# A decoder trunk on one core: the second product of the MLPs by a seven-product scheme in three of four chunks

## The chip, the core and the metric

The kernel runs on one core of one Trainium2 chip. The metric is the device time of one execution in microseconds (us), as the median of several runs. TensorE (PE) multiplies, VectorE (DVE), ScalarE (ACT) and GpSimd (POOL) work on tensors in SBUF, SyncE (SP) issues most DMAs. PSUM has eight banks, each of 128 partitions by 512 float32.

## The reference

The trunk has two layers on 512 tokens of width 1024: attention and retention as token mixers, each followed by a squared-ReLU MLP of width 4096 and a gated embedding. What the change touches is the MLP and what is added behind it:

```python
def sq_relu_mlp(xn, w1, w2):
    h = jax.nn.relu(xn @ w1)
    return (h * h) @ w2
...
        x = x + mix
        x = x + sq_relu_mlp(rms_norm(x, norm_mlp[i]), mlp_w1[i], mlp_w2[i])
        gate = jax.nn.sigmoid(rms_norm(x, norm_pe[i]) @ pe_w_gate[i])
        x = x + gate * (p[i] @ pe_w_up[i])
```

## The kernel before

Activations stand transposed: a tile is 128 features by 512 tokens. Every float32 operand of a product is split into a high half (rounded to the type that TensorE multiplies) and a low half (the remainder); `mm3` makes each product of three passes: high by high (L187), high by low (L188), low by high (L189). A pass loads 128x128 weights and streams 512 columns of tokens.

Weights come through the class `Weights`. `order` lists all weight tiles (128x1024) in the order of their use. `next()` hands out tile i and calls `load()` until four tiles beyond it are under way. `load()` fetches the tile by SP's queue into one of three buffers `raw`, ScalarE casts it to `wh` (L83), VectorE subtracts for the remainder `wl` (L87); of each half there are five buffers. From the first attention products until the middle of the first MLP's first chunk the remainder is made by a DMA instead (`by_dma`).

`mlp` walks over four chunks of 1024 hidden features. In the hidden stage eight tiles of 24 passes go to banks `ph` (three buffers, tag mm). `end` empties a bank: VectorE takes the maximum with 0 times `rsm` (`ht`, L644), ScalarE squares and casts to `hh`, VectorE makes `hl` (L165). In the second product eight output tiles of 24 passes go to banks `py`, and VectorE adds each to the residual `x[m]` (L654). The first chunk of an MLP starts with two tiles side by side, since the row sums for `rsm` come late (`tiles`, `late`).

In each layer the embedding product `p @ pe_w_up` is made early: for layer 0 it waits in DRAM (`up0`) and `back` reads it into `put` by SP's queue; for layer 1 it waits in SBUF, in eight tiles `pus` of the pool `zp`. `gated_embedding` uses it in `end` (L698) and, in the last layer, stores `x[m]` by SP's queue (L701); its last tile goes in two halves of 256 columns.

The order of instructions on each engine is set by a scheduler from the program's order, its buffers and dependencies; each engine then works through its own list strictly in that order.

Of the kernel before, what the change touches and what calls it, by code (L numbers as in the profile page):

```python
# [10 lines left out]
F32 = mybir.dt.float32  # L11
# [5 lines left out]
P = 128  # L17
# [34 lines left out]
class Weights:  # L52
# [3 lines left out]
    def __init__(self, tc, pool, order, ahead):  # L56
        self.tc, self.nc, self.pool, self.order, self.ahead = tc, tc.nc, pool, order, ahead
        self.made = []
        self.at = 0
        self.lo_engines = (self.nc.vector,)  # L60
        self.parts = 1
        self.by_dma = False

    def load(self):
        nc = self.nc
        i = len(self.made)
        src = self.order[i]
        raw = self.pool.tile([P, 1024], F32, name=f"raw{i}", tag="raw", bufs=RAW_BUFS)
# [32 lines left out]
def decoder_trunk(ctx: ExitStack, tc, xT, pT, small, dist, decay, ident,  # L101
# [10 lines left out]
    def ps_mm(name):  # L112
        return psum("mm", 3, name)
# [17 lines left out]
    def gate_order(up, g):  # L131
        return [up[0], up[1]] + [g[i] for i in range(8)]

    order = []
# [5 lines left out]
    for c in range(4):  # L140
        order += [w1_0[8 * c + i] for i in range(8)]
        order += [w2_0[8 * c + i] for i in range(8)]
    order += [w_g0[i] for i in range(8)]
    for h in range(RH):
        order += [w_rv[4 * h + i] for i in range(4)]
# [6 lines left out]
    for c in range(4):  # L152
        order += [w1_1[8 * c + i] for i in range(8)]
        order += [w2_1[8 * c + i] for i in range(8)]
    order += [w_g1[i] for i in range(8)]

    W = Weights(tc, gp, order, W_BUFS - 1)
# [147 lines left out]


    dp = ctx.enter_context(tc.tile_pool(name="dp", bufs=1, space=bass.MemoryType.DRAM))
    up0 = dp.tile([KD // 2, P, 2, T], F32, name="up0")


    with tc.tile_pool(name="at", bufs=1) as ap:
# [314 lines left out]
    def mlp(z, acc, layer, late_at=2):  # L626
        late, rs = rs_rows(acc, f"rsm{layer}")
        nacc = None
        zn = []
        with tc.tile_pool(name=f"mlp{layer}", bufs=1) as mp:  # L630
            for c in range(4):
                hs = []

                def begin(f):
                    if (layer, c, f) == (0, 0, 4):
                        W.by_dma = False
                    return W.next(), ps_mm(f"ph{layer}{c}{f}")

                def unit(s, f, k):
                    mm3(s[1], cols(s[0], slice(k * P, k * P + P)), z[k], k == 0, k == KD - 1)  # L640

                def end(s, f):
# [5 lines left out]
                tiles(8, begin, unit, end, late if c == 0 else None, late_at)  # L648
                for m in range(KD):
                    w = W.next()  # L650
                    ps = ps_mm(f"py{layer}{c}{m}")
                    for f in range(8):
                        mm3(ps, cols(w, slice(f * P, f * P + P)), hs[f], f == 0, f == 7)
                    nc.vector.tensor_tensor(out=x[m], in0=x[m], in1=ps, op=ALU.add)  # L654
                    if c == 3:
                        if m == 0:
                            nacc = slot(f"acc_p{layer}")
                        zn.append(make_z(x[m], C_PE + 8 * layer, m))
                        squares(nacc, x[m], m)
        return zn, nacc  # L660

    def gated_embedding(z, acc, p, layer, last, make=slot, made=None):
# [45 lines left out]
            tiles(KD, begin, unit, end, late)  # L708
        return zn, st["acc"]

    with tc.tile_pool(name="zp", bufs=1) as zp:

        def zslot(name, dt):
            return zp.tile([P, T], dt, name=name, tag="z", bufs=16)

        def back(pool, m):
            t = pool.tile([P, T], F32, name="put", tag="put", bufs=4)
            load(t, up0[m // 2][:, m % 2, :])
            return t

        z, acc = mlp(z, acc, 0)
        z, acc = gated_embedding(z, acc, None, 0, False, zslot, made=back)


        late, rs = rs_rows(acc, "rsr")
        zn = []
        with tc.tile_pool(name="ret", bufs=1) as ap:
# [229 lines left out]
```

## Time and profile before

| | |
|---|---|
| runs, median (lowest to highest) | 1474.82 us (1474.77 to 1479.93), 3 runs |
| the profiled execution, its own time | 1477.73 us |
| its span | 1476.0 us |
| TensorE busy | 1456.2 us (99%), 6668 passes recorded |
| weight loads busy | 1195.0 us (81%) |
| VectorE busy | 787.9 us (53%) |
| ScalarE busy | 648.7 us (44%) |
| GpSimd busy | 155.2 us (11%) |
| chain that ended last, share of TensorE | 91% |

The span is the time from the first to the last instruction in the profiled execution. Busy times are unions, since recorded passes overlap; a TensorE that is busy throughout is not thereby at its peak.

### The profile page before, as it was taken

The numbers are of one execution on the slowest core, as the hardware profiler recorded it, in microseconds if no ns is written. First come the engines' busy times: TensorE is split into PE (matmuls) and PEld (weight loads), VectorE is DVE, ScalarE is ACT, GpSimd is POOL, SyncE is SP. The second block draws the span as 40 slices with busy tenths as digits, with TensorE's granted clock in tenths as the row PEclk, the third lists the DMA queues.
The fourth block names the chain that finished last, engine by engine and source line by source line (L and its number), as shares of the span: only waits on it lengthen the run. The fifth ranks groups of instructions, "written<-read, shape, count | busy, mean of one in ns | idle before, by whom it ended". The sixth has DMA issues, their size and how long they took to land.

```text
span 1476.0 us, 17128 instructions
## 1 busy us (share of the span) xinstructions
PE 1456.2 (99%) x6668; PEld 1195.0 (81%) x6668; DVE 787.9 (53%) x1189; ACT 648.7 (44%) x1007; POOL 155.2 (11%) x127
## 2 busy tenths in 40 slices
PE   9999999999999999999999999999999999999998
PEld 7777667888888888888888888888878888888887
DVE  6776677643434434485464555553684343434455
ACT  6777777742323223354442532433552231323432
POOL 4112112100000000310120200301220000000020
PEclk9999999999999999999999999999999999999999
DMA  6654566853333333244223133142233333333312
GB/s 227 143 115 115 129 170 142 216 158 100 100 90 96 100 101 98 65 152 134 66 88 112 64 101 93 57 129 71 84 102 100 92 94 100 100 98 91 98 58 86
DMA packets 46880, 159.92 MB, mean 108 GB/s; under 512 B 5200, under 2 KB 5712, under 8 KB 46800
## 3 DMA queue, kind: packets, MB, share of 16 engines
q1 hardware_dynamic: 41328, 138.92, 30.1%
q0 software_dynamic: 4896, 17.83, 6.7%
q10 hardware_dynamic: 576, 2.10, 0.4%
q8 instruction: 52, 0.85, 0.2%
q14 instruction: 28, 0.23, 0.0%
HBM read 136.80 MB, written 4.19 MB: 96 GB/s over the span
## 4 chain that ended last, share of the span: by engine, by line
PE 91%; DVE 3%; ACT 2%; DMA 2%; issue 1%; POOL 0%; SPq 0%; ACTq 0%; POOLq 0%; DVEq 0%
PE py L187 8%; PE py L188 8%; PE py L189 8%; PE ph L188 8%; PE ph L187 8%; PE ph L189 8%; PE rg L187 2%; PE rg L188 2%; PE pg L189 2%; PE pg L188 2%; PE pg L187 2%; PE rv L188 2%; PE rqk L188 2%; PE rv L189 2%; PE rqk L189 2%; PE rv L187 2%
## 5 line engine op out<-in xcount | busy, mean ns | idle before, releaser
L83 ACT CAST wh<-raw 128x1024 fp32r<-128x1024 f32 (+1 forms) x211 | 221.0, 1049 | 602.7 <-PE py L188 235.7
L87 DVE TENSOR_TENSOR wl<-raw,wh 128x1024 fp32r<-128x1024 f32 (+1 forms) x211 | 266.8, 1265 | 55.0 <-ACT wh L83 54.0
L188 PE MATMUL ph<-zl,wh 128*128 128x512 f32 x512 | 199.4, 390 | 0.1
L187 PE MATMUL ph<-zh,wh 128*128 128x512 f32 x512 | 199.2, 389 | 0.0
L189 PE MATMUL ph<-zh,wl 128*128 128x512 f32 x512 | 199.2, 389 | 0.0
L187 PE MATMUL py<-hh,wh 128*128 128x512 f32 x512 | 199.2, 389 | 0.0
L188 PE MATMUL py<-hl,wh 128*128 128x512 f32 x512 | 199.2, 389 | 0.0
L189 PE MATMUL py<-hh,wl 128*128 128x512 f32 x512 | 199.2, 389 | 0.0
L654 DVE TENSOR_TENSOR x<-x,py 128x512 f32<-128x512 f32 x64 | 44.0, 688 | 200.0 <-PE py L189 200.0
L644 DVE SCALAR_TENSOR_TENSOR ht<-ph,rsm 128x512 f32<-128x512 f32 x64 | 44.1, 691 | 158.3 <-PE ph L189 158.0
L188 PEld LDWEIGHTS ph<-zl,wh 128*128 128x128 f32 x512 | 96.1, 188 | 20.6 <-DVE zl L168 0.9
L187 PEld LDWEIGHTS ph<-zh,wh 128*128 128x128 f32 x512 | 96.1, 188 | 20.1
L189 PEld LDWEIGHTS py<-hh,wl 128*128 128x128 f32 x512 | 96.1, 188 | 20.1
L189 PEld LDWEIGHTS ph<-zh,wl 128*128 128x128 f32 x512 | 96.1, 188 | 20.0
L187 PEld LDWEIGHTS py<-hh,wh 128*128 128x128 f32 x512 | 96.1, 188 | 20.0
L188 PEld LDWEIGHTS py<-hl,wh 128*128 128x128 f32 x512 | 96.1, 188 | 19.8
L237 POOL TENSOR_TENSOR acc_p<-acc_p,sq 128x512 f32<-128x512 f32 x14 | 24.2, 1726 | 649.0 <-ACT sq L236 649.0
L187 PE MATMUL pqk<-wh,zh 128*128 128x512 f32 x128 | 51.7, 404 | 1.7 <-ACT qkt L368 1.7
L188 PE MATMUL pqk<-wl,zh 128*128 128x512 f32 x128 | 50.9, 398 | 0.8 <-DMA wl<-raw 0.8
L187 PE MATMUL pg<-zh,wh 128*128 128x512 f32 (+1 forms) x136 | 51.2, 377 | 0.0
L189 PE MATMUL pg<-zh,wl 128*128 128x512 f32 (+1 forms) x136 | 51.2, 377 | 0.0
L188 PE MATMUL pg<-zl,wh 128*128 128x512 f32 (+1 forms) x136 | 51.2, 376 | 0.0
(870 smaller groups left out, 2776.8 us busy)
## 6 DMA issues: line engine op xcount, KB each, us to landing
raw<-in_w SPq DMA_DIRECT2D x128, 512.0 KB, 3.6
wl<-raw POOLq DMA_DIRECT2D x34, 512.0 KB, 5.3
raw<-in_w_qk SPq DMA_DIRECT2D x16, 512.0 KB, 3.8
raw<-in_w_g SPq DMA_DIRECT2D x16, 512.0 KB, 3.7
raw<-in_w_rv SPq DMA_DIRECT2D x16, 512.0 KB, 3.7
raw<-in_w_rqk SPq DMA_DIRECT2D x16, 512.0 KB, 4.2
raw<-in_w_rg SPq DMA_DIRECT2D x16, 512.0 KB, 3.6
raw<-in_w_ro SPq DMA_DIRECT2D x16, 512.0 KB, 3.7
```

Of the source, the lines that this page charges most:

```text
L83: nc.scalar.copy(out=hi[:, s], in_=raw[:, s])
L87: e.tensor_tensor(out=lo[:, r], in0=raw[:, r], in1=hi[:, r].bitcast(F32), op=ALU.subtract)
L187: nc.tensor.matmul(ps, a[0], b[0], start=start, stop=False)
L188: nc.tensor.matmul(ps, a[0], b[1], start=False, stop=False)
L189: nc.tensor.matmul(ps, a[1], b[0], start=False, stop=stop)
L237: (engine or nc.gpsimd).tensor_tensor(out=acc, in0=acc, in1=sq, op=ALU.add)
L644: nc.vector.scalar_tensor_tensor(out=t, in0=s[1], scalar=0.0, in1=rs, op0=ALU.max, op1=ALU.mult)
L654: nc.vector.tensor_tensor(out=x[m], in0=x[m], in1=ps, op=ALU.add)
```

## The change

In the first three of four chunks of each MLP the second product is made by a scheme of seven block products for eight. Hidden features, output features and tokens are each cut in two. A round covers four output tiles (two rounds a chunk). Weight blocks are a11, a12, a21, a22 (each 128x1024 here: two tiles j by 512), and

- s1 = a21 + a22 (VectorE), s2 = s1 - a11, s4 = a12 - s2, s3 = a11 - a21 in place of a21 (GpSimd),
- of the hidden activations seven parts of 256 tokens: the four quarters and four sums `hu` (VectorE),
- seven products of 24 passes with 256 columns, accumulated in banks b, c, a; after each product VectorE adds the bank as it stands to a half of an `x` tile.

`MIX` lists the products in their order: name, bank, part of the hidden activations, and the half tile to which the bank is then added. In a chunk's first round the last quarter (q = 3) of s1 and s2 is put behind their other three. The hidden tiles come in pairs (tile f and f + 4). The second layer's embedding product now waits in DRAM (`up1`), stored by ScalarE's queue and read by `back`.

```diff
+MIXED = 3
+MIX = (
+    ("a11", "b", 0, (0, 0)),
+    ("s1", "c", 3, (1, 1)),
+    ("s2", "b", 5, (0, 1)),
+    ("s4", "c", 2, (0, 1)),
+    ("s3", "b", 4, (1, 1)),
+    ("a12", "a", 1, (0, 0)),
+    ("a22", "b", 6, (1, 0)),
+)
...
+    def mixed(self, kind, w, first):
...
+        def fetch(b):
+            raw = self.pool.tile([P, 1024], F32, name=f"raw{i}_{b}", tag="raw", bufs=RAW_BUFS)
+            src = w[first + b // 2 : first + b // 2 + 3 : 2, :, b % 2 * T : b % 2 * T + T].rearrange("j p n -> p j n")
+            self.tc.keep_in_program_order(nc.sync.dma_start(out=raw.rearrange("p (j n) -> p j n", j=2), in_=src))
+            return raw
+
+        def fresh():
+            return self.sums.tile([P, 1024], F32, name=f"mix{i}", tag="mix", bufs=2)
+
+        if kind == "a11":
+            t = mix["a11"] = fetch(0)
+        elif kind == "s1":
+            mix["a21"], a22 = fetch(2), fetch(3)
+            t = mix["s1"] = fresh()
+            nc.vector.tensor_tensor(out=t, in0=mix["a21"], in1=a22, op=ALU.add)
+        elif kind == "s2":
+            t = mix["s2"] = fresh()
+            nc.gpsimd.tensor_tensor(out=t, in0=mix["s1"], in1=mix["a11"], op=ALU.subtract)
+        elif kind == "s4":
+            mix["a12"] = fetch(1)
+            t = fresh()
+            nc.gpsimd.tensor_tensor(out=t, in0=mix["a12"], in1=mix["s2"], op=ALU.subtract)
+        elif kind == "s3":
+            t = mix["a21"]
+            nc.gpsimd.tensor_tensor(out=t, in0=mix["a11"], in1=t, op=ALU.subtract)
+        elif kind == "a12":
+            t = mix["a12"]
+        else:
+            t = fetch(3)
+        hi = self.pool.tile([P, 1024], F32R, name=f"wh{i}", tag="wh", bufs=W_BUFS)
+        lo = self.pool.tile([P, 1024], F32R, name=f"wl{i}", tag="wl", bufs=W_BUFS)
+        nc.scalar.copy(out=hi, in_=t)
+        nc.vector.tensor_tensor(out=lo, in0=t, in1=hi.bitcast(F32), op=ALU.subtract)
+        return hi, lo
...
+            def products(n, j, first, last):
+                kind, b, part, (tile, half) = MIX[n]
...
+                ps = bank[b, j][:, 0 : T // 2]
+                for q in range(first, last):
+                    mm3(
+                        ps, cols(ws[n], slice(j * T + q * P, j * T + q * P + P)),
+                        tuple(p[:, part, :] for p in hs[q]), n == opens[b] and q == 0, q == 3, n != opens[b],
+                    )
+                if last == 4:
+                    t = x[4 * r + 2 * j + tile][:, half * (T // 2) : (half + 1) * (T // 2)]
+                    nc.vector.tensor_tensor(out=t, in0=t, in1=ps, op=ALU.add)
...
-                    t = mp.tile([P, T], F32, name="ht", tag="ht", bufs=3)
-                    nc.vector.scalar_tensor_tensor(out=t, in0=s[1], scalar=0.0, in1=rs, op0=ALU.max, op1=ALU.mult)
-                    nc.scalar.activation(out=t, in_=t, func=AF.Square)
-                    hs.append(hilo(mp, "h", t, bufs=10))
...
+                    if c >= MIXED:
+                        put(2 * second, 2, half)
+                    elif not second:
+                        put(0, 1, t[:, 0:1, :])
+                    else:
+                        put(1, 2, half)
+
+                        u = mp.tile([P, 4, T // 2], F32, name="hu", tag="hu", bufs=1)
+                        nc.vector.tensor_tensor(out=u[:, 0:2, :], in0=t[:, 1:4:2, :], in1=t[:, 0:2, :], op=ALU.subtract)
+                        nc.vector.tensor_tensor(out=u[:, 2, :], in0=t[:, 3, :], in1=u[:, 0, :], op=ALU.subtract)
+                        nc.vector.tensor_tensor(out=u[:, 3, :], in0=t[:, 2, :], in1=u[:, 2, :], op=ALU.subtract)
+                        put(3, 4, u)
...
-                t = zslot(f"pus{m}", F32)
                 nc.scalar.copy(out=t, in_=pu)
-                made.append(t)
+                nc.scalar.dma_start(out=up1[m // 2][:, m % 2, :], in_=t)
...
-        gated_embedding(z, acc, None, 1, True, made=lambda pool, m: made[m])
+    gated_embedding(z, acc, None, 1, True, made=back(up1))
```

Three places show how the lists of instructions change. The first is VectorE's list in the hidden stage of the first MLP's second chunk (chunk 1), from tile 5 to tile 7 (`ph015` to `ph017`); before:

```order
L644 SCALAR_TENSOR_TENSOR ht_3803<-ph015_3778,rsm0_3005 128x512
L87 TENSOR_TENSOR wl60_3812<-raw60_3810,wh60_3811 128x1024
L165 TENSOR_TENSOR hl_3807<-ht_3803,hh_3806 128x512
L644 SCALAR_TENSOR_TENSOR ht_3841<-ph016_3816,rsm0_3005 128x512
L87 TENSOR_TENSOR wl61_3850<-raw61_3848,wh61_3849 128x1024
L165 TENSOR_TENSOR hl_3845<-ht_3841,hh_3844 128x512
L644 SCALAR_TENSOR_TENSOR ht_3879<-ph017_3854,rsm0_3005 128x512
```

and now:

```order
L233 TENSOR_TENSOR hl_3993<-ht_3991,hh_3992 128x256
L759 SCALAR_TENSOR_TENSOR ht_3991<-ph015_4008,rsm0_3003 128x512
L145 TENSOR_TENSOR wl66_4046<-mix66_4043,wh66_4045 128x1024
L777 TENSOR_TENSOR hu_4037<-ht_3991 128x512
L233 TENSOR_TENSOR hl_3993<-ht_3991,hh_3992 128x512
L778 TENSOR_TENSOR hu_4037<-ht_3991,hu_4037 128x256
L779 TENSOR_TENSOR hu_4037<-ht_3991,hu_4037 128x256
L233 TENSOR_TENSOR hl_3993<-hu_4037,hh_3992 128x1024
L759 SCALAR_TENSOR_TENSOR ht_4074<-ph016_4049,rsm0_3003 128x512
L145 TENSOR_TENSOR wl67_4086<-mix67_4083,wh67_4085 128x1024
L233 TENSOR_TENSOR hl_4076<-ht_4074,hh_4075 128x256
L759 SCALAR_TENSOR_TENSOR ht_4074<-ph017_4089,rsm0_3003 128x512
```

Between the evictions of tiles 5 and 6 stand six operations where there were two; wl66 and wl67 are the halves of s2 and s4, whose inputs GpSimd makes.

The second is VectorE's list in the second product of that chunk; before, additions to x and weight remainders alternate:

```order
L654 TENSOR_TENSOR x1_2318<-x1_2318,py011_3924 128x512
L87 TENSOR_TENSOR wl64_3952<-raw64_3950,wh64_3951 128x1024
L654 TENSOR_TENSOR x2_2403<-x2_2403,py012_3956 128x512
L87 TENSOR_TENSOR wl65_3984<-raw65_3982,wh65_3983 128x1024
L654 TENSOR_TENSOR x3_2462<-x3_2462,py013_3988 128x512
```

and now, where round one (`py010`) goes over into round two (`py011`; b, c, a and 0, 1 in the names are the bank and the output tile j):

```order
L127 TENSOR_TENSOR mix72_4257<-raw72_2_4253,raw72_3_4255 128x1024
L720 TENSOR_TENSOR x3_2463<-x3_2463,py010b1_4143 128x256
L720 TENSOR_TENSOR x0_2269<-x0_2269,py010a0_4295 128x256
L145 TENSOR_TENSOR wl72_4260<-mix72_4257,wh72_4259 128x1024
L145 TENSOR_TENSOR wl73_4292<-mix73_4289,wh73_4291 128x1024
L720 TENSOR_TENSOR x2_2404<-x2_2404,py010a1_4309 128x256
L720 TENSOR_TENSOR x1_2319<-x1_2319,py010b0_4129 128x256
L720 TENSOR_TENSOR x3_2463<-x3_2463,py010b1_4143 128x256
L145 TENSOR_TENSOR wl74_4328<-mix74_4325,wh74_4327 128x1024
L145 TENSOR_TENSOR wl75_4359<-raw72_2_4253,wh75_4358 128x1024
L720 TENSOR_TENSOR x4_2507<-x4_2507,py011b0_4362 128x256
L720 TENSOR_TENSOR x6_2604<-x6_2604,py011b1_4376 128x256
```

The additions of a12 and a22 (`py010a1`, `py010b0`, `py010b1`) stand behind wl73, the addition of round two's first product behind wl74 and wl75. wl72, wl73 and wl74 are made from s1 (mix72), s2 (mix73) and s4 (mix74); GpSimd's own list makes mix73, then s3 in place of raw72_2, then mix74.

The third is SP's list of fetches, with what each waits for; before, one fetch per weight tile:

```order
L82 DMA raw60_3810<-in_w2_0 128x1024 [waits DMAHW2_49,DVE_49]
L82 DMA raw61_3848<-in_w2_0 128x1024 [waits DMAHW3_49,DVE_49]
L82 DMA raw62_3886<-in_w2_0 128x1024 [waits DMAHW4_49,DVE_49]
L82 DMA raw63_3918<-in_w2_0 128x1024 [waits DMAHW5_49,DVE_49]
L82 DMA raw64_3950<-in_w2_0 128x1024 [waits DMAHW6_49,DVE_49]
```

and now, from a12 of round one to a12 of round two:

```order
L116 DMA raw67_1_4081<-in_w2_0 128x2x512 [waits DMAHW7_49,DVE_49]
L116 DMA raw70_3_4181<-in_w2_0 128x2x512 [waits DVE_49,DMAHW5_49,Activation_49,Pool_49]
L116 DMA raw71_0_4221<-in_w2_0 128x2x512 [waits DMAHW6_49,DVE_49]
L116 DMA raw72_2_4253<-in_w2_0 128x2x512 [waits DMAHW0_49,DVE_49,Pool_49]
L116 DMA raw72_3_4255<-in_w2_0 128x2x512 [waits DMAHW1_49,DVE_49]
L116 DMA raw74_1_4323<-in_w2_0 128x2x512 [waits DMAHW4_49,DVE_49]
```

Five fetches make seven weight tiles; raw72_3 takes the buffer of raw70_3 and so waits for VectorE's remainder wl70.

## Rows read from the trace of the kernel before

**Rows 1.** The table of stretches: length, then PE, PEld, DVE, ACT, POOL busy (count); clock.

```profile
404.00:448.00 44.00, 44.00 (x196) 36.44 (x195) 15.96 (x17) 9.59 (x10) 0.00 (x0) 1.00 0.33 98
```

**Rows 2.** The groups by line and shape, TensorE; busy us, mean ns of one, idle before.

```profile
L187 PE MATMUL py<-hh,wh 128*128 128x512 f32 x512 | 199.2, 389 | 0.0
```

**Rows 3.** The timeline of TensorE near the end; start us, us, instruction.

```profile
1459.84 0.39 PE L187 MATMUL pg<-zh,wh 128*128 128x512 f32 x1
...
1465.28 0.28 PE L187 MATMUL pg<-zh,wh 128*128 128x256 f32 x1
...
1465.40 0.19 PEld L189 LDWEIGHTS pg<-zh,wl 128*128 128x128 f32 x1
...
1470.91 0.28 PE L189 MATMUL pg<-zh,wl 128*128 128x256 f32 x1
```

**Rows 4.** The timeline of VectorE and ScalarE at a hidden tile of the first MLP.

```profile
367.71 1.05 ACT L83 CAST wh<-raw 128x1024 fp32r<-128x1024 f32 x1 [4.39 <-PE ph L188]
...
367.94 0.69 DVE L644 SCALAR_TENSOR_TENSOR ht<-ph,rsm 128x512 f32<-128x512 f32 x1 [3.35 <-PE ph L189]
...
368.67 0.62 ACT L645 ACTIVATE ht<-ht 128x512 f32<-128x512 f32 x1
...
368.80 1.23 DVE L87 TENSOR_TENSOR wl<-raw,wh 128x1024 fp32r<-128x1024 f32 x1 [0.17 <-ACT wh L83]
```

**Rows 5.** The groups by line and shape, VectorE and ScalarE, 1455 to 1476 us.

```profile
L696 DVE TENSOR_TENSOR gt<-pg,rsp 128x256 f32<-128x256 f32 x2 | 0.8, 425 | 1.1 <-PE pg L189 1.1
...
L697 ACT ACTIVATE gt<-gt 128x256 f32<-128x256 f32 x2 | 0.8, 417 | 4.4 <-DVE gt L696 4.4
```

**Rows 6.** The timeline of GpSimd, VectorE and ScalarE in the retention's first head.

```profile
743.38 3.98 POOL L845 TENSOR_TENSOR ro<-ro,rt 128x512 f32<-128x512 f32 x2 [11.12 <-DVE ro L842]
...
743.88 2.32 DVE L87 TENSOR_TENSOR wl<-raw,wh 128x1024 fp32r<-128x1024 f32 x1
...
745.15 0.62 ACT L164 CAST goh<-ro 128x512 fp32r<-128x512 f32 x1 [0.51 <-POOL ro L845]
...
746.12 1.78 DVE L842 SCALAR_TENSOR_TENSOR ro<-ro,sm,ror 128x512 f32<-128x512 f32 x1
...
747.39 0.62 ACT L164 CAST goh<-ro 128x512 fp32r<-128x512 f32 x1 [1.62 <-POOL ro L845]
...
747.83 0.68 DVE L165 TENSOR_TENSOR gol<-ro,goh 128x512 fp32r<-128x512 f32 x1
...
748.43 0.68 DVE L807 TENSOR_TENSOR rt<-rg,rsr 128x512 f32<-128x512 f32 x1
```

**Rows 7.** The groups by line and shape, GpSimd.

```profile
L845 POOL TENSOR_TENSOR ro<-ro,rt 128x512 f32<-128x512 f32 x16 | 30.6, 1923 | 53.0 <-DVE ro L842 50.2 <-ACT goh L164 2.8
...
L237 POOL TENSOR_TENSOR oacc<-oacc,sq 128x512 f32<-128x512 f32 x12 | 15.5, 1290 | 273.0 <-ACT sq L236 273.0
```

**Rows 8.** The DMA issues (KB each, us to landing); last, put's landing times.

```profile
raw<-in_w SPq DMA_DIRECT2D x128, 512.0 KB, 3.6
...
p<-in_pT SPq DMA_DIRECT2D x2, 512.0 KB, 4.5
...
put<-up SPq DMA_DIRECT2D x1, 256.0 KB, 2.9
...
DMA to landing us min/median/max: 2.6/4.0/6.8
```

**Rows 9.** The timeline of VectorE at the start of the first MLP.

```profile
288.02 1.29 DVE L644 SCALAR_TENSOR_TENSOR ht<-ph,rsm 128x512 f32<-128x512 f32 x2
```

**Rows 10.** The timeline of SP and VectorE in the last gate.

```profile
1442.33 0.94 SPq L701 DMA_DIRECT2D out_xT<-x  x2
...
1445.11 0.69 DVE L698 TENSOR_TENSOR gt<-pus,gt 128x512 f32<-128x512 f32 x1 [0.70 <-ACT gt L697]
...
1472.13 0.42 DVE L698 TENSOR_TENSOR gt<-pus,gt 128x256 f32<-128x256 f32 x1 [0.48 <-ACT gt L697]
```

**Rows 11.** The timeline of ScalarE's queue at layer 0's embedding product.

```profile
256.67 0.34 ACTq L590 DMA_DIRECT2D up<-pus  x1
```

More of the change, by code (lines that the diff above doesn't have):

```diff
@@ L62, in __init__ @@
         self.by_dma = False
+        self.mix = {}
+        self.sums = None
     def load(self):
@@ L67, in load @@
         src = self.order[i]
+        if isinstance(src, tuple):
+            self.made.append(self.mixed(*src))
+            return
         raw = self.pool.tile([P, 1024], F32, name=f"raw{i}", tag="raw", bufs=RAW_BUFS)
@@ L132, in gate_order, with mlp_order, hidden_order @@
         return [up[0], up[1]] + [g[i] for i in range(8)]
+    def mlp_order(w1, w2):
+        o = []
+        for c in range(4):
+            o += [w1[8 * c + f] for f in hidden_order(c)]
+            if c < MIXED:
+                o += [(kind, w2, 8 * c + 4 * r) for r in range(2) for kind, _, _, _ in MIX]
+            else:
+                o += [w2[8 * c + i] for i in range(8)]
+        return o
+    def hidden_order(c):
+        return [f + 4 * a for f in range(4) for a in range(2)] if c < MIXED else list(range(8))
     order = []
@@ L139, in decoder_trunk @@
     order += [w_o[i] for i in range(6)] + [w_up0[0], w_o[6], w_o[7], w_up0[1]]
-    for c in range(4):
-        order += [w1_0[8 * c + i] for i in range(8)]
-        order += [w2_0[8 * c + i] for i in range(8)]
+    order += mlp_order(w1_0, w2_0)
     order += [w_g0[i] for i in range(8)]
@@ L151, in decoder_trunk @@
     order += [w_ro[4 * RH - 4 + i] for i in range(4)]
-    for c in range(4):
-        order += [w1_1[8 * c + i] for i in range(8)]
-        order += [w2_1[8 * c + i] for i in range(8)]
+    order += mlp_order(w1_1, w2_1)
     order += [w_g1[i] for i in range(8)]
@@ L307, in decoder_trunk @@
     dp = ctx.enter_context(tc.tile_pool(name="dp", bufs=1, space=bass.MemoryType.DRAM))
-    up0 = dp.tile([KD // 2, P, 2, T], F32, name="up0")
+    up0, up1 = (dp.tile([KD // 2, P, 2, T], F32, name=f"up{i}") for i in range(2))
     with tc.tile_pool(name="at", bufs=1) as ap:
@@ L629, in mlp, with mix_round @@
         zn = []
+        opens = {b: n for n, (_, b, _, _) in reversed(list(enumerate(MIX)))}
+        made_by = {"b": ps_mm, "c": ps_s, "a": ps_tr}
+        def mix_round(c, r, hs):
+            bank = {}
+            ws = {}
+            def products(n, j, first, last):
+                kind, b, part, (tile, half) = MIX[n]
+                if n not in ws:
+                    ws[n] = W.next()
+                if (b, j) not in bank:
+                    bank[b, j] = made_by[b](f"py{layer}{c}{r}{b}{j}")
+                ps = bank[b, j][:, 0 : T // 2]
[7 more added lines that the diff above has]
+                    nc.vector.tensor_tensor(out=t, in0=t, in1=ps, op=ALU.add)
+            n = 0
+            if r == 0:
+                for j in range(2):
+                    products(0, j, 0, 4)
+                for n in (1, 2):
+                    for j in range(2):
+                        products(n, j, 0, 3)
+                for n in (1, 2):
+                    for j in range(2):
+                        products(n, j, 3, 4)
+                n = 3
+            for n in range(n, len(MIX)):
+                for j in range(2):
+                    products(n, j, 0, 4)
@@ L640, in unit, with end, put @@
                     mm3(s[1], cols(s[0], slice(k * P, k * P + P)), z[k], k == 0, k == KD - 1)
-                def end(s, f):
-                    t = mp.tile([P, T], F32, name="ht", tag="ht", bufs=3)
-                    nc.vector.scalar_tensor_tensor(out=t, in0=s[1], scalar=0.0, in1=rs, op0=ALU.max, op1=ALU.mult)
-                    nc.scalar.activation(out=t, in_=t, func=AF.Square)
-                    hs.append(hilo(mp, "h", t, bufs=10))
+                def end(s, i):
+                    second = i % 2
+                    if not second:
+                        st["t"] = mp.tile([P, 4, T // 2], F32, name="ht", tag="ht", bufs=2)
+                        hs.append([mp.tile([P, 7, T // 2], F32R, name=f"h{part}", tag=f"h{part}", bufs=4) for part in "hl"])
+                    t = st["t"]
+                    half = t[:, 2 * second : 2 * second + 2, :]
+                    nc.vector.scalar_tensor_tensor(
+                        out=half, in0=s[1].rearrange("p (a n) -> p a n", a=2), scalar=0.0,
+                        in1=rs.rearrange("p (a n) -> p a n", a=2), op0=ALU.max, op1=ALU.mult,
+                    )
+                    nc.scalar.activation(out=half, in_=half, func=AF.Square)
+                    h = hs[-1]
+                    def put(a, n, src):
+                        split_into(h[0][:, a : a + n, :], h[1][:, a : a + n, :], src)
+                    if c >= MIXED:
+                        put(2 * second, 2, half)
+                    elif not second:
+                        put(0, 1, t[:, 0:1, :])
+                    else:
+                        put(1, 2, half)
[4 more added lines that the diff above has]
+                        put(3, 4, u)
@@ L648, in mlp @@
                 tiles(8, begin, unit, end, late if c == 0 else None, late_at)
+                if c < MIXED:
+                    for r in range(2):
+                        mix_round(c, r, hs)
+                    continue
                 for m in range(KD):
@@ L714, in zslot, with back, made @@
             return zp.tile([P, T], dt, name=name, tag="z", bufs=16)
[L716 to L722, printed above, removed]
+        def back(up):
+            def made(pool, m):
+                t = pool.tile([P, T], F32, name="put", tag="put", bufs=4)
+                load(t, up[m // 2][:, m % 2, :])
+                return t
+            return made
+        z, acc = gated_embedding(z, acc, None, 0, False, zslot, made=back(up0))
         late, rs = rs_rows(acc, "rsr")
```

29 lines of the change are left out of this document (17 added, 12 removed).

## The prediction

> **What bounds the kernel now.** The table of stretches comes first: through one second product of the first MLP TensorE is busy 44.00 of 44.00 us at granted clock 1.00, VectorE 15.96, ScalarE 9.59, GpSimd not at all [rows 1]. TensorE sets the time and every other engine has slack, so time is won only by less work on TensorE, and only while nothing makes it wait. The groups by line then give the amount: three kinds of 512-wide passes, 512 of each [rows 2], 1536 in 8 chunks, so 192 a chunk. Their 389 ns overlap; the pitch comes from starts in the timeline. From 1459.84 to 1465.28 lie 24 passes of 512 columns, 0.2267 us each; from 1465.28 to the start of the 48th pass of 256 columns at 1470.91 are 47 pitches, 0.1198 us each, with one weight load a pass beside them [rows 3]. Halving the columns costs 13 ns a pair, no more.
>
> **The products.** A round of the scheme is 7 products of 24 passes, two rounds a chunk: 336 of 256 columns for 192 of 512. TensorE's listing has 7455 rows for 6591, 864 more, which is 6 times 144, so the change does what it says. Per chunk 336 x 0.1198 = 40.25 us for 192 x 0.2267 = 43.53, a gain of 3.28; for six chunks **-19.7 us**, the most there is to win.
>
> The Trainium skill (TensorE: Matmul & The Clock Gate, Back-to-back issue gap) puts a sustained pass at 81 ns for 128 columns and 131 ns for 512. By that page, as an estimate, a 256-wide pass is at least 0.62 of a 512-wide one, a chunk 336 x 0.62 x 0.2267 = 47.2 us, and the six would lose 22 us where the sum here has them gain 19.7. The trace disagrees: 0.1198 to 0.2267 is 0.53.
>
> **What the other engines must deliver.** A weight pair is now used up in 2.88 us instead of 5.44. VectorE takes 1.23 us for 1024 columns, 0.69 for 512 [rows 4], 0.42 for 256 [rows 5]; in a full queue the next operation starts 0.08 before the recorded end (747.83 and 0.68, next 748.43 [rows 6]), so 1.15, 0.61, 0.34. ScalarE takes 1.05, 0.63, 0.42 [rows 4, 5]. GpSimd's sums are new: 1024 wide, two inputs. The nearest rows are 512 wide, 1.29 us alone and 1.92 beside VectorE [rows 7]. Bounds are 1.3 (if all were fixed cost) and 3.85 (twice 1.92); I take twice 1.29, 2.6, since the 1.92 contains waiting that I count apart.
> That waiting is in [rows 6]. GpSimd's two products from 743.38 to 747.36 and VectorE's operations on two SBUF tensors go one at a time: the weight remainder, issued at 743.88, ends 1.1 after ScalarE got GpSimd's first result (745.15) and lasts 2.32 for 1.23; GpSimd's second result comes at 747.39, and the product issued at 746.12 ends only after it, 1.78 for 0.74. An operation that reads PSUM (748.43) is not held. So the two engines take turns, a whole instruction each. Almost all new VectorE work has two SBUF inputs; each of three sums a round holds it up to 2.6 us.
>
> **Hidden stage into round one** (chunk 1 of the first MLP; clock 0 at its first pass, tile i ends at 5.44(i+1)). The remainder wl63 ends at 19.3: its cast waits for tile 2 (16.3) and a 1024-wide cast. It frees a raw buffer, the load takes 3.6 [rows 8], s1's sum runs 22.95 to 24.2. From there to the low half of tile 6 (hl_4076), for which TensorE waits, VectorE has six operations of 1024, four of 512, six of 256 and three evictions: 6 x 1.15 + 7 x 0.61 + 6 x 0.34 = 13.2 us. GpSimd's three sums come between, 7.8, less 0.7 that lies beside an eviction; twice VectorE waits for a 1024-wide cast, 1.7 in all. 24.2 + 13.2 + 7.8 - 0.7 + 1.7 is 46.2, to its end 46.4. TensorE asks at 43.52 + 10 x 0.12 = 44.7: it waits 1.7. Behind that row stand tile 7's eviction (to 47.05), two remainders, four sums, two x additions and hl of the last pair, to 53.1, asked for at 52.5: 0.6 more. **2.3 us a chunk.** Before, the same place had only hl 512 wide after each eviction and no wait.
>
> **Round one into round two** (clock 0 at round one's first pass, those waits left out). The cast of a22 (wh70) waits for s1's last pass at 7.9; its remainder ends at 10.4 behind four x additions. Only this frees the buffer of raw72_3, the sixth fetch with three buffers: it lands at 14.0, s1's sum runs 14.1 to 15.3. GpSimd's s2 runs 15.4 to 18.0; wl72 is held by it and runs to 19.1; s3 has the next turn, to 21.7; wl73, whose cast was ready at 19.0, is held to 22.9; s4 then runs to 25.5. Behind wl73 stand the x additions of a12 and a22, the first of a22 ends at 23.7. It frees the bank in which round two's second half product should start at 21.6: 2.1 us of waiting. Next, wl74 (cast 25.5 to 26.6) and wl75 end at 29.0, and behind them the x addition of round two's first product ends at 29.4; s2's product wants that bank at 28.0: 1.4. **3.5 us a chunk.**
> Later in round two an x addition stands directly behind its product, and no sum runs: no wait.
>
> **The rest.** In the first chunk of the first MLP the remainders made by DMA hold the raw buffers longer and its first evictions start only at 288.02 [rows 9], so the sums lie nearer the end of the stage: 2.5 more (0 to 5). The final gate now loads put from DRAM on SP's queue behind the stores: put 2 stands behind the stores of x0 and x1 (1442.33 and 0.94 us), and is used at 1445.11 [rows 10]. From one x to the next is store and issue 0.45, landing 2.6 to 4.0, 2.9 when alone [rows 8], and 1.4 of VectorE: 4.45 to 5.85, against 5.44 of a tile. At 2.9 the start's lateness heals. The last put is asked for 3.4 us after the last 512-wide tile (1465.28; four steps of 0.63 to 0.69 and a store's issue), at 1468.7, and lands at 1471.6, before the last half tile's use at 1472.13: 0.5 for the first half's queueing. At 4.0 it would be 5.6. Eight DMA issues of 0.34 on ScalarE's queue for up1 [rows 11] lie beside six passes a tile (1.36 us) and its copy; uncovered they would be 2.7.
>
> **Sum.** -19.7 + 6 x (2.3 + 3.5) + 2.5 + 0.5 = +18.1. The profiled execution took 1477.73 us (span 1476.0), so 1495.8; the median of the runs, 1474.82, is 2.9 below it, so **1493 us**. Each 0.1 us on a sum is worth about 0.6 a chunk, each 0.1 on a landing 0.1. Sums of 2.4 to 2.9 and landings of 3.6 to 4.5 [rows 8] make the waits 4.6 to 8.5 a chunk, so, with the 0 to 5 and the tail, 1485 to 1509. With sums at 1.3 the waits vanish (1456), at 3.85 they are 13.5 a chunk (1539); the row without hindrance is nearest, so neither end is likely.
>
> **Rivals.** *GpSimd does not hold VectorE here.* Then the hidden stage ends in time, and in round two only s4's lateness is left, 1.2 a chunk: 6 x (1.2 - 3.28) + 0.5 = -12, 1463 us. It decides from the point where waits fall under 3.28 a chunk. For it: twelve GpSimd additions took 1.29 on average, so without waiting [rows 7]; against it: three VectorE operations of [rows 6]. 0.18.
> *The waits just eat the gain,* 2.1 to 4.4 a chunk, as with sums of 2.0 or a luckier order of turns: 1468 to 1482. 0.19.
> *The weight loads set the pace* in long runs of 256-wide passes: 336 x 0.19 [rows 3] = 63.8 us a chunk, +122, 1597 us. Against it: 48 passes in a row at 0.1198. 0.03.
> *The forecast*: 0.60.
>
> **Numbers.** A measurement of this kernel tells 0.5%, 7.4 us, from no change. Faster 0.18, same 0.19, slower 0.60 + 0.03 = 0.63. The range goes from 1462, so that most of the first rival is in, to 1509, the upper end of the forecast's own range; 0.17 is left out.
>
> **What would show it.** Right: pitch 0.12 in both rounds; GpSimd's sums near 2.6 and VectorE's remainders beside them over 2; TensorE idle near 2 us at the fourth block of a chunk's first product (on hl or hh), and in round two's first and third products on x additions; VectorE near 90% busy in round one. Wrong: no TensorE gaps over 1 us (first rival); a pitch above 0.15; a granted clock under 1.00 after the gaps, which would add to every chunk; gaps in the final gate on put.

## The result, and the profile after

The changed kernel takes **1488.12 us** (median of 5 runs, 1484.54 to 1491.28) against 1474.82 (median of 5, 1474.19 to 1479.93): a ratio of 1.0083, 95% interval 1.0057 to 1.0109. It is slower, as forecast, and 5 us nearer to the old time than the 1493 of the forecast. The profiled execution took 1491.28 us, span 1489.5.

The page of the changed kernel, busy times and the chain that ended last:

```profile
PE 1445.8 (97%) x7532; PEld 1222.9 (82%) x7532; DVE 972.3 (65%) x1453; ACT 704.0 (47%) x1067; POOL 258.9 (17%) x163
...
PE 60%; DVE 18%; DMA 6%; issue 6%; ACT 6%; POOL 3%; SPq 0%; POOLq 0%; DVEq 0%; ACTq 0%
```

TensorE is busy 10 us less than before in a span 13.5 us longer: it waits now. The chain of waits, 91% TensorE before, has only 60% of it, and 18% of VectorE. GpSimd's 104 us more are the new sums.

Where the 13.5 us are is read from the starts of TensorE's passes in the timeline (the last column is the first experiment below; where two numbers stand, they are the two rounds of a chunk):

| stretch, us | before | after | sums on VectorE |
|---|---|---|---|
| start to the first MLP's first hidden pass | 274.76 | 276.00 | 275.32 |
| first MLP, first chunk's second product | 43.52 | 25.76 + 22.82 = 48.58 | 21.00 + 20.21 = 41.21 |
| the five other changed chunks, mean of their two rounds | 43.52 | 21.39 + 23.08 = 44.47 | 20.15 + 20.22 = 40.37 |
| end of the first MLP to the second's first hidden pass | 453.36 | 454.31 | 454.33 |
| end of the second MLP to the span's end | 49.27 | 50.69 | 49.89 |

The differences to before are 1.2, 5.1, 5 x 0.95, 1.0 and 1.4, together 13.4. The first of them is no part of the change: up to that place all the programs have the same instructions on every engine, and in the twelve profiled executions of this study the stretch took 269.1 to 276.6 us. So stretches are compared below, and spans only by the medians of runs.

The table of stretches, for both rounds of the first and of the second chunk of the first MLP (columns: busy us and instructions of PE, PEld, DVE, ACT, POOL; granted clock; DMA share, GB/s):

```profile
320.02:345.78 25.76, 22.17 (x170) 21.76 (x168) 21.97 (x32) 10.60 (x13) 4.65 (x2) 0.93 0.26 82
345.78:368.60 22.82, 20.62 (x170) 20.25 (x169) 17.27 (x25) 8.18 (x8) 4.42 (x2) 1.00 0.54 160
412.15:433.51 21.36, 20.92 (x169) 20.31 (x168) 18.54 (x27) 9.43 (x11) 4.42 (x2) 1.00 0.32 99
433.51:456.58 23.07, 20.64 (x171) 20.27 (x170) 17.41 (x25) 8.18 (x8) 4.65 (x2) 1.00 0.49 158
```

Against [rows 1] VectorE has gone from 36% to 75 to 87% of the stretch, and TensorE is no longer busy throughout. A round without a wait would be 168 passes at 0.12, 20.15 us (so it is in the experiments). TensorE's waits by what ended them (us in total, times, longest; a pass of 256 columns is recorded 0.16 longer than the 0.12 from its start to the next, so each wait is really that much longer):

```profile
PE py111b L255 <- DVE x L720: 3.1, 2, 2.3
PE py000b L255 <- ACT hh L232: 2.7, 1, 2.7
...
PE py011b L255 <- DVE x L720: 2.4, 2, 1.5
...
PE py000b L256 <- DVE hl L233: 0.9, 1, 0.9
...
PE pu L255 <- ACT pus L1008: 0.7, 1, 0.7
...
PE py110b L255 <- ACT hh L232: 0.3, 1, 0.3
...
PE py010c L256 <- DVE hl L233: 0.2, 1, 0.2
```

The digits behind py are layer, chunk and round, counted from 0, and the letter is the bank. Round two's bank b waits for x additions in all six chunks (2.0 to 3.1 us). At the end of the hidden stage only the first chunk of the first MLP waits long (2.7 and 0.9); the five others wait a few tenths each.

What VectorE does meanwhile, in the timeline (start us, us), with GpSimd's sums, in the last hidden tiles of chunk 1 of the first MLP:

```profile
393.01 2.72 POOL L130 TENSOR_TENSOR mix<-mix,raw 128x1024 f32<-128x1024 f32 x1 [42.81 <-DVE mix L127]
...
393.39 2.89 DVE L233 TENSOR_TENSOR hl<-ht,hh 128x512 fp32r<-128x512 f32 x1
...
395.69 2.84 POOL L137 TENSOR_TENSOR raw<-raw,raw 128x1024 f32<-128x1024 f32 x1
...
396.20 2.62 DVE L778 TENSOR_TENSOR hu<-ht,hu 128x256 f32<-128x256 f32 x1
...
403.90 2.47 POOL L134 TENSOR_TENSOR mix<-raw,mix 128x1024 f32<-128x1024 f32 x1 [5.37 <-DVE wl L145]
...
404.62 2.83 DVE L145 TENSOR_TENSOR wl<-mix,wh 128x1024 fp32r<-128x1024 f32 x1
```

And in the same chunk's round one, the same timeline:

```profile
429.09 2.41 POOL L130 TENSOR_TENSOR mix<-mix,raw 128x1024 f32<-128x1024 f32 x1 [22.72 <-DVE mix L127]
...
430.12 5.79 DVE L145 TENSOR_TENSOR wl<-mix,wh 128x1024 fp32r<-128x1024 f32 x2 [0.31 <-ACT wh L144]
...
431.45 3.39 POOL L137 TENSOR_TENSOR raw<-raw,raw 128x1024 f32<-128x1024 f32 x1
...
434.80 3.36 POOL L134 TENSOR_TENSOR mix<-raw,mix 128x1024 f32<-128x1024 f32 x1
...
436.18 0.74 DVE L720 TENSOR_TENSOR x<-x,py010b 128x256 f32<-128x256 f32 x2
```

GpSimd's L130 is s2, L137 is s3, L134 is s4. Beside s2 the low half hl takes 2.89 us where 512 columns take 0.69 [rows 4], beside s3 a sum of 256 columns 2.62 for 0.42 [rows 5], beside s4 a remainder 2.83 for 1.22. In round one two remainders take 5.79 us for 2.4, and behind them stand the x additions of 436.18, which free the bank that round two waits for.

By groups (busy us, mean ns, idle before):

```profile
L130 POOL TENSOR_TENSOR mix<-mix,raw 128x1024 f32<-128x1024 f32 x12 | 30.2, 2516 | 338.6 <-DVE mix L127 317.6
L145 DVE TENSOR_TENSOR wl<-mix,wh 128x1024 fp32r<-128x1024 f32 x36 | 75.8, 2105 | 16.2 <-ACT wh L144 15.8
...
L145 DVE TENSOR_TENSOR wl<-raw,wh 128x1024 fp32r<-128x1024 f32 x48 | 58.0, 1218 | 1.1 <-ACT wh L144 1.1
```

The remainders of the sums, which come beside the sums, average 2.1 us; those of plain blocks 1.22.

The two small losses: at the end of retention TensorE waits for a copy of the embedding product, in the last gate VectorE waits for put. The timelines of ScalarE at the one place, before and after, and of VectorE at the other, with what VectorE's operations on put waited for in all (us, times):

```profile
1047.55 1.07 ACT L867 COPY pus<-pu 128x512 f32<-128x512 f32 x2
```

```profile
1058.63 0.62 ACT L232 CAST goh<-ro 128x512 fp32r<-128x512 f32 x1 [2.38 <-POOL ro L987]
1059.16 1.07 ACT L1008 COPY pus<-pu 128x512 f32<-128x512 f32 x2
```

```profile
1485.03 0.43 DVE L837 TENSOR_TENSOR gt<-put,gt 128x256 f32<-128x256 f32 x1 [1.26 <-DMA put<-up]
...
  DMA put<-up: 9.9, 6
```

The copy at 1059.16 frees TensorE's bank; it stands behind goh's cast, which waited 2.38 us for GpSimd. Before, two copies ran ahead of that cast (1047.55); now only one does.

### The profile page after: what moved, and what is told of

The parts are those of the page before. It is cut to its first block, busy times and chain, and to the rows that moved or that the text cites. A ratio compares the mean times of both kernels' runs of the same rounds, so it can differ in the third digit from the quotient of the medians.

```text
span 1489.5 us, 19352 instructions
## 1 busy us (share of the span) xinstructions
PE 1445.8 (97%) x7532; PEld 1222.9 (82%) x7532; DVE 972.3 (65%) x1453; ACT 704.0 (47%) x1067; POOL 258.9 (17%) x163
## 4 chain that ended last, share of the span: by engine, by line
PE 60%; DVE 18%; DMA 6%; issue 6%; ACT 6%; POOL 3%; SPq 0%; POOLq 0%; DVEq 0%; ACTq 0%
DVE wl L145 4%; DVE hl L233 3%; PE ph L256 3%; PE ph L255 3%; DMA raw<-in_w 3%; PE ph L257 3%; PE rv L255 2%; PE rqk L257 2%; PE rqk L255 2%; PE rv L257 2%; PE py L257 2%; PE py L255 2%; PE py L256 2%; PE rv L256 2%; PE rqk L256 2%
## 5 line engine op out<-in xcount | busy, mean ns | idle before, releaser
L101 ACT CAST wh<-raw 128x1024 fp32r<-128x1024 f32 (+1 forms) x163 | 170.2, 1046 | 361.9 <-PE ph L256 86.1
L105 DVE TENSOR_TENSOR wl<-raw,wh 128x1024 fp32r<-128x1024 f32 (+1 forms) x163 | 208.3, 1279 | 57.9 <-ACT wh L101 56.8
L130 POOL TENSOR_TENSOR mix<-mix,raw 128x1024 f32<-128x1024 f32 x12 | 30.2, 2516 | 338.6 <-DVE mix L127 317.6
L145 DVE TENSOR_TENSOR wl<-mix,wh 128x1024 fp32r<-128x1024 f32 x36 | 75.8, 2105 | 16.2 <-ACT wh L144 15.8
L144 ACT CAST wh<-mix 128x1024 fp32r<-128x1024 f32 x36 | 37.8, 1050 | 90.0 <-DVE mix L127 41.2
L144 ACT CAST wh<-raw 128x1024 fp32r<-128x1024 f32 x48 | 49.1, 1047 | 27.9 <-PE ph L256 10.3
L145 DVE TENSOR_TENSOR wl<-raw,wh 128x1024 fp32r<-128x1024 f32 x48 | 58.0, 1218 | 1.1 <-ACT wh L144 1.1
L232 ACT CAST hh<-hu 128x1024 fp32r<-128x1024 f32 x24 | 25.2, 1050 | 66.9 <-DVE hu L779 66.9
L94 POOL DMA_DIRECT2D wl<-raw x34 | 29.6, 872 | 136.8 <-ACT wl L93 126.0
L257 PE MATMUL pqk<-wh,zl 128*128 128x512 f32 x128 | 51.4, 402 | 0.0
```

What stands on the lines that cost most here:

```text
L130: nc.gpsimd.tensor_tensor(out=t, in0=mix["s1"], in1=mix["a11"], op=ALU.subtract)
L144: nc.scalar.copy(out=hi, in_=t)
L145: nc.vector.tensor_tensor(out=lo, in0=t, in1=hi.bitcast(F32), op=ALU.subtract)
L257: nc.tensor.matmul(ps, a[1], b[0], start=False, stop=stop, skip_group_check=on)
```

## The experiments

The theory: GpSimd's sums and VectorE's operations on two SBUF tensors take turns, so VectorE's queue runs late both at the end of the hidden stage and between the rounds, and TensorE's waits are more than the shorter passes save. Rivals: VectorE simply has too much to do (V); the first sum of a round comes late because its operand waits for one of three raw buffers (B).

**Sums on VectorE.**

```diff
-            nc.gpsimd.tensor_tensor(out=t, in0=mix["s1"], in1=mix["a11"], op=ALU.subtract)
+            nc.vector.tensor_tensor(out=t, in0=mix["s1"], in1=mix["a11"], op=ALU.subtract)
```

and so for s4 and s3.

> All three GpSimd sums of a round (s2, s3, s4) on VectorE instead. Theory (GpSimd and VectorE take turns, so each sum keeps VectorE's queue waiting 2.5 to 3.1 us): a sum then costs VectorE 1.15 us, 1.4 to 2 less than it is held now; the 2.7 us of TensorE waiting between round one and two fall to about 0.5 a chunk, the 1.0 at the end of the hidden stage to 0, and the first chunk's 5.1 us of loss to 1 or 2: about 1465 us (1461 to 1470). Rival V (VectorE simply has too much to do): 3.45 us a round more work on it, waits grow, about 1500 us. Rival B (the sixth fetch waits for one of three raw buffers, so the first sum of round two is late): round two's waits stay, only the hidden stage's go, about 1482 us.

Measured: **1461.02 us**, ratio to before 0.989 (0.9872 to 0.9908). Moving 36 additions to the busier engine turns 13 us of loss into 14.8 of gain. The table of stretches for chunk 1 of the first MLP, two groups, and the start of s1's sum in that chunk's round one:

```profile
404.10:424.25 20.15, 20.15 (x170) 20.15 (x168) 17.40 (x27) 8.37 (x9) 0.00 (x0) 1.00 0.34 105
424.25:444.41 20.16, 20.16 (x171) 20.16 (x169) 16.65 (x25) 8.30 (x8) 0.00 (x0) 1.00 0.60 178
```

```profile
L145 DVE TENSOR_TENSOR wl<-mix,wh 128x1024 fp32r<-128x1024 f32 x36 | 43.8, 1216 | 0.2 <-ACT wh L144 0.2
...
L134 DVE TENSOR_TENSOR mix<-raw,mix 128x1024 f32<-128x1024 f32 x12 | 14.6, 1216 | 0.0
```

```profile
418.42 1.23 DVE L127 TENSOR_TENSOR mix<-raw,raw 128x1024 f32<-128x1024 f32 x1 [0.75 <-DMA raw<-in_w]
```

TensorE is busy throughout. Although VectorE makes three sums more a round, it is busy 16.7 of 20.2 us in round two where it was busy 17.4 of 23.1, and 956 us in all instead of 972. Rival V falls. So does B, by which round two's waits would have stayed: s1's sum still waits for its load and starts 14.3 us after the round's first pass, as late as in the changed kernel when that round's own 1.2 us of waits are left out (15.6), and TensorE waits for nothing.

**No sums on GpSimd at all.** s1, a21 and a12 as they are stand in for s2, s3 and s4, so the result lacks these sums.

```diff
-            t = mix["s2"] = fresh()
-            nc.gpsimd.tensor_tensor(out=t, in0=mix["s1"], in1=mix["a11"], op=ALU.subtract)
+            t = mix["s2"] = mix["s1"]
```

and so for s4 and s3.

> s2, s3 and s4 are left out (s2 uses s1, s3 uses a21, s4 uses a12 as they are), so the result lacks these sums; passes, casts, remainders and s1's addition stay. Theory: the waits of both places vanish, what is left is the gain of the passes (19.7 us) less some 1.4 in the last gate, 0.9 at the end of retention and about 0.2 a round: 1459 us (1456 to 1464). Rival V: the same order, 1460. Rival B: the waits of round two stay at about 2 us a chunk, 1472 us.

Measured: 1458.24 us, ratio 0.9881 (0.9863 to 0.9899). All twelve rounds take 20.15 or 20.16 us: six chunks come to 241.9 us for 261.1, so the passes save 19.3 us. The sums on VectorE come within 3 us of that.

**One more raw buffer** for s1's second operand.

```diff
+            if kind == "s1" and b == 3:
+                raw = self.sums.tile([P, 1024], F32, name=f"raw{i}_{b}", tag="more", bufs=1)
+            else:
+                raw = self.pool.tile([P, 1024], F32, name=f"raw{i}_{b}", tag="raw", bufs=RAW_BUFS)
```

> The second operand of s1 (a22) gets a buffer of its own beside the three of raw, so its load waits for no other tile of the round. Theory (turns): s1's sum of round two starts some 3 us earlier, but the three sums hold VectorE as before, now in round one; waits of round two go from 2.7 to about 1 us a chunk, those at the hidden stage stay: about 1478 us (1472 to 1484). Rival B: the waits of round two vanish, 1470 us. Rival V: no change, 1488 us.

Measured: 1500.31 us, ratio 1.0164 (1.0146 to 1.0182): slower than any of the three theories had it. The hidden stage's waits do vanish in four of the five later chunks (round one 20.15), but round two grows from 23.1 to some 25.9. The timeline of chunk 1, first round:

```profile
425.56 5.36 DVE L148 TENSOR_TENSOR wl<-mix,wh 128x1024 fp32r<-128x1024 f32 x2
...
429.80 3.36 POOL L137 TENSOR_TENSOR mix<-raw,mix 128x1024 f32<-128x1024 f32 x1
...
434.27 1.23 DVE L148 TENSOR_TENSOR wl<-mix,wh 128x1024 fp32r<-128x1024 f32 x1 [2.69 <-ACT wh L147]
435.41 0.75 DVE L723 TENSOR_TENSOR x<-x,py010b 128x256 f32<-128x256 f32 x2
...
435.88 0.58 PE L258 MATMUL py011b<-hh,wh 128*128 128x256 f32 x1 [3.50 <-DVE x L723]
```

s1's sum starts 12.1 us after the round's first pass instead of 15.6, as B wanted, and the remainders beside the sums are held as before. But the scheduler now puts the x additions of round one's last product (435.41) behind the remainder of s4 (434.27), which waits for GpSimd's third sum; TensorE waits 3.5 us for them in every chunk. A granted clock of 0.5 follows (see the last section).

To see whether the buffer itself costs anything, it was run with the sums on VectorE:

> The extra raw buffer of the run at 1500.3 us, with the three sums on VectorE. Reading of that run's trace: with the buffer, the additions to x of round one's last product stand behind the remainder of s4, and that waits for GpSimd's third sum; the 12 us above the changed kernel are GpSimd's sums, in another place. Then with the sums on VectorE nothing is left of them: 1461 us (1458 to 1464), as without the buffer. If the buffer costs by itself (loads that come earlier and collide, or its place in SBUF): 1470 us or more.

Measured: 1461.08 us, ratio 0.9907 (0.9881 to 0.9933). The buffer costs nothing and gives nothing; what it changed was where GpSimd's lateness is felt.

**Idle work on GpSimd.** The sums on VectorE are both shorter and out of GpSimd's way. This run separates the two: beside each stands an addition on GpSimd that nobody uses.

```diff
+            mix["idle"] = self.sums.tile([P, 1024], F32, name=f"idle{i}", tag="idle", bufs=2)
+            nc.gpsimd.tensor_tensor(out=mix["idle"], in0=mix["s1"], in1=mix["s1"], op=ALU.add)
```

> The sums on VectorE as in the run at 1461.0 us, and beside each of s2, s3, s4 an addition of the same size on GpSimd whose result nobody uses (the first reads s1, the others the one before). The sums are no longer late for GpSimd's sake, so this separates the two effects of GpSimd's sums. If the turns make the loss (each idle addition keeps VectorE from its two-input operations for 2.4 to 3.4 us): VectorE's remainders beside them take over 2 us again, and the waits come back, larger than in the changed kernel since VectorE now makes the sums too: 1485 to 1515 us. If only the lateness of GpSimd's results made it: 1461 us, no change.

Measured: **1513.16 us**, ratio 1.025 (1.0224 to 1.0275): 52 us for 36 additions whose results nobody waits for. The timeline of chunk 1, first round:

```profile
429.54 1.89 POOL L132 TENSOR_TENSOR idle<-mix 128x1024 f32<-128x1024 f32 x1 [30.65 <-DVE mix L127]
...
429.65 2.87 DVE L130 TENSOR_TENSOR mix<-mix,raw 128x1024 f32<-128x1024 f32 x1
...
431.52 2.76 POOL L138 TENSOR_TENSOR idle<-idle 128x1024 f32<-128x1024 f32 x1
...
432.44 2.91 DVE L153 TENSOR_TENSOR wl<-mix,wh 128x1024 fp32r<-128x1024 f32 x1
...
434.35 2.76 POOL L144 TENSOR_TENSOR idle<-idle 128x1024 f32<-128x1024 f32 x1
...
435.27 0.41 DVE L728 TENSOR_TENSOR x<-x,py010a 128x256 f32<-128x256 f32 x1
...
435.61 2.58 DVE L153 TENSOR_TENSOR wl<-mix,wh 128x1024 fp32r<-128x1024 f32 x1
```

The two engines alternate: VectorE's sum ends 1.09 after GpSimd's first addition, GpSimd's second ends 1.8 after that, VectorE's remainder 1.07 later, and so on. The x addition at 435.27, one of whose inputs is in PSUM, runs in its usual 0.41 us during GpSimd's third. Nor does VectorE wait here for a buffer or a result: by groups, it never stands idle before the remainders of the sums, which average 1.8 us in place of 1.22:

```profile
L153 DVE TENSOR_TENSOR wl<-mix,wh 128x1024 fp32r<-128x1024 f32 x36 | 65.5, 1818 | 0.0
```

Held time alone thus makes a loss of this kind and more; some 11 of the 52 us are passes at half clock behind TensorE's longer waits (see the last section). Late results of GpSimd can add to it, as the run with the buffer shows. The Trainium skill (SBUF — State Buffer, Who interferes with whom) says that a VectorE instruction with two SBUF inputs contends with a GpSimd instruction that reads SBUF, and calls the port pair that the two share an exclusive lock. The trace agrees, at 2.58 to 2.91 us for 1.22.

**Idle copies** in place of the idle additions (`tensor_copy` of the same tiles).

> As the run with idle GpSimd additions (1513.2 us), but the three idle GpSimd instructions of a round are copies: one input instead of two, the same 1024 columns. If any GpSimd instruction on SBUF takes a turn, VectorE's additions and remainders beside the copies take over 2 us again and the time is near 1500 us (less than 1513 if copies are shorter than additions). If only instructions with two inputs from SBUF take turns on both sides, VectorE's stay at 1.2 us and the time is 1461 us, that of the sums on VectorE alone.

Measured: 1480.11 us, ratio 1.0023 (1.0007 to 1.0038), 19 us above the sums on VectorE, between the two expectations. The timeline of chunk 1, first round:

```profile
421.50 1.04 POOL L132 COPY idle<-mix 128x1024 f32<-128x1024 f32 x1 [30.91 <-DVE mix L127]
...
421.61 2.00 DVE L130 TENSOR_TENSOR mix<-mix,raw 128x1024 f32<-128x1024 f32 x1
...
422.60 1.91 POOL L138 COPY idle<-idle 128x1024 f32<-128x1024 f32 x1
...
423.54 2.05 DVE L153 TENSOR_TENSOR wl<-mix,wh 128x1024 fp32r<-128x1024 f32 x1
```

The profiled execution took 1475.29 us, 4.8 below the median. Copies take turns too: the two copies shown cost VectorE 0.8 us each and the third 0.5 (the next remainder takes 1.72), where an addition costs 1.4 to 1.7. So a second input on GpSimd's side is not needed; what VectorE loses goes with the length of GpSimd's instruction (1.04 us for the first copy, 1.89 for the first addition).

**The embedding product in DRAM alone**, in the kernel before.

```diff
-                made.append(t)
+                nc.scalar.dma_start(out=up1[m // 2][:, m % 2, :], in_=t)
```

> The kernel before with only one part of the change: the second layer's embedding product waits in DRAM, written by ScalarE's queue and read back by SP's. If this move alone makes the 1.4 us that the last gate is longer in the changed kernel and the 0.9 us wait at the end of retention: 1477.1 us against 1474.8. If those come from the scheme's other transfers and not from the move: 1474.8 us.

Measured: 1479.55 us against 1475.79, ratio 1.0022 (1.0009 to 1.0035). The stretch between the MLPs is 454.37 us (453.36 before), the last 50.12 (49.27): 1.9 us from the move alone. The other part of the difference is in the stretch before the first MLP, where nothing was changed (276.61).

**Two repairs on top of the sums on VectorE.**

```diff
-                nc.scalar.dma_start(out=up1[m // 2][:, m % 2, :], in_=t)
+                nc.sync.dma_start(out=up1[m // 2][:, m % 2, :], in_=t)
...
+            ready = [made(ap, m) for m in range(KD)] if last else None
...
-                t = pool.tile([P, T], F32, name="put", tag="put", bufs=4)
+                t = pool.tile([P, T], F32, name="put", tag="put", bufs=8)
```

> The sums on VectorE, and two repairs around the embedding product in DRAM: its stores go by SP's queue in place of ScalarE's, and the last gate asks for all eight put tiles at its start, ahead of its own stores (eight buffers). If the 1.0 us at the end of retention comes from the issues on ScalarE's queue and the 0.6 to 1.4 us in the last gate from put standing behind the stores, both go: 1459.3 us against 1461.0. If the stores on SP's queue hold up the weight loads behind them, or eight put loads do so at the start of the gate: 1461 to 1465.

> The same kernel as vector_sums_early_put again, in one call with the sums on VectorE alone. From the traces the two repairs are worth 1.9 us (1.0 at the end of retention, 0.9 in the last gate), so 1459.2 against 1461.0; if the first comparison was chance, both come out alike.

> The sums on VectorE again, as the partner of vector_sums_early_put_2: 1461 us, 1.9 above it; if the first comparison was chance, both come out alike.

Measured: 1459.48 us, ratio 0.9884 (0.9866 to 0.9902), then **1458.05** (1456.39 to 1459.13), ratio 0.988 (0.9866 to 0.9894), beside 1461.32 (1459.35 to 1464.35), ratio 0.9907 (0.9892 to 0.9922). By the medians the repairs are worth 1.5 and 3.3 us; the ratios' intervals overlap, in the second pair by a hair, so the medians alone do not settle it. The stretches, from the first of the two traces, show them: 453.32 us between the MLPs (454.33 without), 49.02 in the last gate (49.89), 1.9 us together. The tile put in the last gate, second run (duration of an issue in ns, first and last start in us; below it, what VectorE's operations on put waited for):

```profile
L183 SPq DMA_DIRECT2D put<-up x8: 327/430/433, 1408.5 to 1411.7; - x8
...
  ACT gt L837: 3.8, 6
```

All eight loads are issued from 1408.5 to 1411.7, and VectorE waits for none; in the changed kernel it waited for put six times, 9.9 us in all. This version beats both kernels: 1.2% below the kernel before, 30 us below the changed one.

## Why the prediction was right, step by step

**The products: right.** A round without waits takes 20.15 us for 168 passes, 0.120 each, and the six chunks save 19.3 us of the forecast 19.7. The estimate of 47.2 us a chunk by the Trainium skill (TensorE: Matmul & The Clock Gate, Back-to-back issue gap) does not hold here: 40.31 was measured where no sum was made by GpSimd.

**GpSimd's sums and the turns: right.** Taken at 2.6 us, they average 2.5 for s2 and, with their own waiting, 3.0 and 3.1 for s4 and s3. That they hold VectorE, read from three operations of [rows 6], is shown by the idle additions. The rival with 0.18, that GpSimd does not hold VectorE, falls with them.

**Hidden stage into round one: right in kind, too large.** Forecast 2.3 us a chunk; round one is 21.39 for 20.15, 1.2. The walk held to within 0.1 us as far as s1's sum (clock 22.95 forecast, 391.65 less 368.60 = 23.05 measured). The term that was too large is the hold: "GpSimd's three sums come between, 7.8, less 0.7". The three held operations lost 2.2, 2.2 and 1.6 us, 6.0 in all. Part of each sum lay beside the operation that VectorE had begun before it.

**Round one into round two: nearly right.** Forecast 2.1 + 1.4 = 3.5 us; round two is 23.08 for 20.16, 2.9. In chunk 1 the two waits are 1.7 and 1.1, at the named places, on x additions behind remainders.

**The first chunk: the size by luck.** Forecast 2.5 us more than another chunk, measured 48.58 - 44.47 = 4.1. It waits 2.9 and 1.2 us on the last hidden tiles, and then runs 16 passes at half the clock (1.5 us). The sum did not have this; the prediction named a lower clock behind the gaps as a sign of being wrong in every chunk, and it came in this one alone. Since the other terms were too large and this one too small, the chunk as a whole came out at 8.3 us over 40.31, as forecast.

**The end of retention: wrong by 1.0.** The step that failed counts the issues as lying "beside six passes a tile (1.36 us) and its copy". The issues themselves do, but with them a copy stands behind goh's cast, which waits for GpSimd, and TensorE waited for the copy's bank; with the stores on SP's queue two copies run ahead of the cast again, and the loss is gone. The step left out ScalarE's order around goh.

**The last gate: 0.5 forecast, 1.4 measured.** The last put was asked for 1 us later than the walk had it (1481.8; 1468.7 plus the 12.1 us by which the gate starts later is 1480.8), and was used at 1485.03, 3.2 us after it was asked for where the walk had a landing of 2.9.

**The sum.** Forecast +18.1 on the profiled execution; the stretches give 13.4, or 12.2 without the one ahead of the first MLP: 18.1 + 0.4 (passes) - 5 x 1.64 (waits of the later chunks) + 1.0 (retention) + 0.9 (last gate). The first chunk adds nothing to this, since its errors cancel. Errors of both signs thus cancel in part, and some of the nearness of 1488 to 1493 is luck. The range of 1485 to 1509 is worked out from the waits alone (6 x 4.6 and 6 x 8.5 in place of 6 x 5.8); with the first chunk's 0 to 5 and the tail's 5.1 at the late landing, which it says that it holds, it would be some 1483 to 1517. The rival in which the waits "just eat the gain" (1468 to 1482) is 6 us away from the measured 1488; that weight loads set the pace (1597) is excluded by the 20.15 us of a round.

## What to carry to other kernels

Work that is moved to an idle GpSimd is not free for VectorE: in these traces a VectorE operation with two SBUF inputs that comes up while GpSimd works on SBUF waits for the end of GpSimd's instruction. Compare what an operation costs VectorE itself (1.22 us here) with what its GpSimd form takes from VectorE's queue (1.6 to 2.2), and count the operations behind it that TensorE waits for; the busier engine was here the better place by 27 us. And when a wait is read as the lack of a buffer, look at what else stands in that queue: here the extra buffer only moved the wait, behind s4's remainder.

## What was not expected of the hardware

A wait of TensorE can cost more than its length. After waits of 2.9 and 1.2 us in the first chunk the granted clock is at 1.2 GHz for a while; the same in the run with one more raw buffer, after 3.5 us of waiting (the table of stretches, TensorE, of the changed kernel, then of that run):

```profile
325.23:328.72 3.49, 3.49 (x17) 0.52 0.20 39
330.00:333.00 3.00, 3.00 (x27) 1.00 0.32 94
```

```profile
435.40:442.30 6.90, 6.42 (x31) 0.51 0.33 88
442.30:450.00 7.70, 7.70 (x67) 1.00 0.44 144
```

At granted clocks of 0.52 and 0.51, that is at 1.2 GHz, passes of 256 columns come every 0.213 us instead of 0.12. In the run with the buffer 27 passes went so, 2.5 us on top of a wait of 3.65. The waits of 1.1 to 2.4 us in the other rounds of the changed kernel were followed by no such drop and cost only their length. In the run with the buffer each of the six waits of 3.65 us between the rounds was followed by one, and round two took 5.0 to 6.5 us more than without a wait. In the run with idle copies a wait of 2.7 us that ended at 1230.4, in the second MLP, was followed by one as well (granted clock 0.56 from 1230.4 to 1234.0). What decides it was not tried.
